# Attention on one core: the order of the next batch's K and Q chunks, and an addition moved from GpSimd to DMA

## The chip, the cores and the metric

The kernel runs on one core of a Trainium2 chip. A core has a matrix engine (TensorE, in the profile PE for matmuls and PEld for the loading of weights), three engines for element-wise work (VectorE, DVE; ScalarE, ACT; GpSimd, POOL), a synchronisation engine (SP) that here only issues DMAs, and 16 DMA engines that all queues share. The engines run their instruction streams in order and wait for each other by semaphores.

The metric is the device time of one execution in microseconds. The kernel before took 791.19 us in the median of three runs (790.79, 791.19 and 791.87).

## The reference

Eight independent batches of softmax attention, 2048 queries and keys, 512 wide, float32 in and out:

```python
scores = np.matmul(q, k.transpose(0, 2, 1)) / np.sqrt(d_k)     # q, k, v: (8, 2048, 512)
attn_weights = special.softmax(scores, axis=-1).astype(np.float32)
return np.matmul(attn_weights, v)
```

## The kernel before

Both matrix products are computed in float16 by Strassen-Winograd recursion: seven products of half-sized blocks instead of eight, with the sums of blocks made by DVE. For the scores the blocks of K are 4 chunks of 512 rows (K0 to K3, the tiles `kraw`), of Q 4 chunks too (two of them form one "sp", half of a batch's queries). For the product with V there is a second level for three of the seven products (class `Fine`, the function `fine`).

**Periods and slots.** The main loop runs over 32 periods g, four to a batch (qt = g % 4, called first to fourth period here). A period has 28 slots, and a slot holds two 512-column score matmuls for the queries to come, together with PV matmuls for the period itself. Everything is laid out by hand by (period, slot): `PRODUCTS` says at which slot a PV product is issued, `SUMS` at which slot DVE gets a sum (`k01@11` is the first sum of chunk K0 at slot 11 of the second period, `q1@25` the first sum of the next queries, `k31@1` the first of K3 in the fourth), and `PLAN` at which slot the next batch's inputs are loaded and transposed. A slot is a place in the engines' instruction streams, not a clock: what stands there may wait.

**Inputs of the next batch.** `load` (L133) is a DMA on the POOL queue that converts 512 rows from float32 in memory to float16 in a tile `stage`; there are two such tiles, so a third load waits until the transposition of the first has finished. `dma_transpose` (L159) is a transposing DMA on the SP queue from `stage` into `kraw` or `qraw`; it waits for its load and until PE has read the old contents for the last time. `load_v` (L220) loads V on the POOL queue. With K's chunks c and j the sums of K are at L194 to L197, those of Q at L211 to L214, of V at L228 to L231, and those for the second level at L602 to L605.

**Outputs.** A period ends in two row blocks, a and b, of four parts each, C11, C12, C21 and C22 (`o11`, `o12`, `o21`, `o22`), 128 x 256 float32 in tiles `o`. There are eight such tiles, and a new one is whichever has come free first. ACT scales a product out of PSUM into an `o` (L460), DVE may add a second part (L463), and SP sends the store (L473). C22 and C21 are finished by products a7, b7, a4 and b4 at the beginning of the next period, C12 by a6 and b6 in slots 19 to 24. C11 is the sum of two scaled parts, done at slots 25 and 27 (`after2`):

```python
way = ADDERS[self.g % NQT]
...
more = self.half()
self.scaled(more, self.y[:, 0:H], self.r1)
if way == "dma":
    nc.gpsimd.dma_start(out=self.o11, in_=more, accum_op=ADD)
    stores.append((clock[0] + LAG, lambda: self.store(self.o11, 0, slice(0, H))))
    return
nc.gpsimd.tensor_add(self.o11, self.o11, more)
```

In the form "pool" POOL adds the parts (L569) and the store follows at once; in the form "dma" a DMA on the POOL queue adds one tile onto the other in place (L564), and the store is put on SP's queue LAG slots later, where it waits for that DMA. The last two periods of all have no scores and no C11 of this kind.

**Queues.** SP's queue carries all stores and all transposing DMAs in the order of the slots, POOL's all loads, the additions and the accumulating DMAs. Each is in order: an instruction that waits holds what stands behind it.

Of the kernel before, what the change touches and what calls it, by code (L numbers as in the profile page):

```python
# [12 lines left out]
def kernel(  # L13
# [394 lines left out]
    spare_halves = deque()  # L408
    stores = deque()
    clock = [0]  # L410
    LAG = 12
    ADDERS = ("pool", "pool", "dma", "dma")

    class Pair:

# [109 lines left out]
    class Fine(Pair):  # L525
# [29 lines left out]
        def after2(self):  # L555
            if "y" in INNER(self.g) and self.g < NP - 2:
                way = ADDERS[self.g % NQT]
                if way == "dve":
                    self.final(self.o11, self.y[:, 0:H], self.r1)
                else:  # L560
# [4 lines that stand above are left out]
                        stores.append(  # L565
                            (clock[0] + LAG, lambda: self.store(self.o11, 0, slice(0, H)))
                        )
# [124 lines left out]
    def INNER(g):  # L692
        return INNERS[g % NQT] if 0 < g < NP - 2 else END_INNERS.get(g, "")
# [69 lines left out]
    PLAN = {}  # L763
    for qt_, slot_, *what_ in (
# [10 lines left out]
    ):  # L775
        PLAN.setdefault((qt_, slot_), []).append(what_)
# [229 lines left out]
```

## Time and profile before

| | |
|---|---|
| median of three runs | 791.19 us (790.79 to 791.87) |
| profiled execution, its own time | 790.61 us |
| its span, first to last instruction | 788.8 us |
| granted TensorE clock, mean | 1.000 |
| PE busy | 782.1 us, 99% of the span |
| DVE busy | 704.8 us, 89% |
| ACT busy | 645.8 us, 82% |
| POOL busy | 125.9 us, 16% |
| memory read and written | 100.73 MB and 33.55 MB |
| C11 added by POOL (L569) | 30 instructions, mean 936 ns |
| C11 added by DMA (L564) | 28 issues of 128 KB, 3.4 us to landing in the median |

The profile is of one execution. A line of a timeline reads: start in us from the first instruction, duration, engine, line of the kernel, operation, what it writes and reads, shape, how many are merged, and in brackets how long the engine stood idle before and what ended that. "SPq" and "POOLq" are entries of a queue rather than work of an engine. A line of the chain of waits has start, length and what ran, or which DMA was waited for. A line "DMA to landing" has the least, median and longest time from issue to landing. A matmul's duration overlaps with the next one's, so steps are read from starts, not from durations.

### The profile page before, as it was taken

To read this page: it belongs to the slowest core of one execution; us is meant where nothing else is said; L and a number is where in the kernel's file an instruction comes from. 1 tells how busy PE (TensorE), PEld (TensorE's weight loads), DVE (VectorE), ACT (ScalarE), POOL (GpSimd) and SP (SyncE) were. 2 spreads that over 40 slices of the span, in tenths; PEclk is the share of its full clock that TensorE was granted. 3 is DMA by queue.
4 is the path that set the end of the run, shared out by engine and by line. 5 is a ranking of instruction groups with operands and counts; after the bars stand their busy time and mean duration, and the time that the engine had idled before them with its cause. 6 is when DMAs were issued, how large, how long until landed. Compare 5 with 4: busy or idle time off the path is not lost.

```text
span 788.8 us, 17985 instructions
## 1 busy us (share of the span) xinstructions
PE 782.1 (99%) x6574; PEld 536.9 (68%) x6574; DVE 704.8 (89%) x1562; ACT 645.8 (82%) x1339; POOL 125.9 (16%) x166
## 2 busy tenths in 40 slices
PE   9999999999999999999999999999999999999998
PEld 5556666666667666666666676676666666667686
DVE  3789999989999899997999989999899988999864
ACT  4678888888888988888888888888888878888852
POOL 4011111121121120211202121022210222100000
PEclk9999999999999999999999999999999999999999
DMA  9999991999939998499966999579992999922112
GB/s 222 182 150 161 181 205 42 195 194 165 196 50 206 199 178 146 84 200 173 185 136 112 191 202 166 111 141 184 188 202 68 160 191 185 175 74 61 49 67 94
DMA packets 210488, 119.73 MB, mean 152 GB/s; under 512 B 124768, under 2 KB 209376, under 8 KB 210400
## 3 DMA queue, kind: packets, MB, share of 16 engines
q0 software_dynamic: 53680, 52.96, 45.4%
q1 hardware_dynamic: 156432, 65.30, 40.2%
q8 instruction: 51, 0.84, 0.4%
q10 hardware_dynamic: 288, 0.33, 0.1%
q14 instruction: 37, 0.30, 0.1%
HBM read 100.73 MB, written 33.55 MB: 170 GB/s over the span
## 4 chain that ended last, share of the span: by engine, by line
PE 96%; DVE 1%; DMA 1%; ACT 1%; issue 0%; DVEq 0%; ACTq 0%
PE t L342 45%; PE t L451 30%; PE t L648 17%; PE t L285 2%; DMA kraw<-stage 1%; PE tr L169 1%; PE t L867 0%; PE tr L146 0%; PE t L301 0%; DVE s L396 0%; DVE cz L367 0%; ACT left L278 0%; ACT o L460 0%; DVE s L398 0%; ACT right L278 0%
## 5 line engine op out<-in xcount | busy, mean ns | idle before, releaser
L460 ACT ACTIVATE o<-t,r 128x256 f32<-128x256 f32 x314 | 143.6, 479 | 84.6 <-DVE r L486 29.6
L342 PE MATMUL t<-qraw,kraw 128*128 128x512 f16 x728 | 198.0, 379 | 0.1
L278 ACT ACTIVATE left<-t 128x512 f16<-128x512 f32 (+1 forms) x260 | 154.2, 600 | 11.7 <-PE t L342 4.7
L342 PE MATMUL t<-qs,ks 128*128 128x512 f16 x488 | 138.7, 379 | 0.1
L278 ACT ACTIVATE right<-cz 128x1024 f16<-128x1024 f32 x122 | 129.8, 1064 | 1.0 <-DVE cz L364 0.8
L342 PEld LDWEIGHTS <-kraw 128*128 128x128 f16 x976 | 87.1, 97 | 57.9 <-issue 0.8
L451 PEld LDWEIGHTS <-right 128*128 128x128 f16 x1024 | 99.6, 98 | 36.3 <-issue 1.5
L451 PEld LDWEIGHTS <-s 128*128 128x128 f16 x1072 | 102.2, 97 | 29.8 <-issue 0.3
L648 PEld LDWEIGHTS <-si 128*128 128x128 f16 x1044 | 76.0, 97 | 38.4 <-DVE si L605 2.5
L342 PEld LDWEIGHTS <-ks 128*128 128x128 f16 x732 | 67.9, 97 | 40.2 <-issue 0.2
L367 DVE TENSOR_TENSOR cz<-t,cz 128x512 f32<-128x512 f32 x122 | 83.5, 685 | 12.0 <-PE t L342 4.1
L358 ACT COPY cz<-t 128x512 f32<-128x512 f32 x120 | 70.4, 587 | 27.0 <-PE t L342 25.5
L364 DVE TENSOR_TENSOR cz<-t,cz 128x512 f32<-128x512 f32 x122 | 83.3, 683 | 6.0 <-PE t L342 5.5
L648 PEld LDWEIGHTS <-left 128*128 128x128 f16 x928 | 66.2, 97 | 20.6
L463 DVE SCALAR_TENSOR_TENSOR o<-t,r,o 128x256 f32<-128x256 f32 x134 | 62.4, 477 | 18.1 <-ACT ci L666 7.2
L353 ACT COPY t<-t 128x512 f32<-128x512 f32 x120 | 70.0, 583 | 3.2 <-PE t L342 0.8
L451 PE MATMUL t<-vt,s 128*128 128x256 f16 (+1 forms) x560 | 72.5, 272 | 0.0
L342 PE MATMUL t<-qs,kraw 128*128 128x512 f16 x244 | 72.5, 378 | 0.0
L342 PE MATMUL t<-qraw,ks 128*128 128x512 f16 x244 | 72.5, 378 | 0.0
L361 ACT COPY cz<-t 128x512 f32<-128x512 f32 x122 | 71.1, 582 | 0.4
L648 PE MATMUL t<-vh,left 128*128 128x128 f16 x696 | 67.3, 219 | 0.0
L451 PE MATMUL t<-vh,s 128*128 128x257 f16 x512 | 67.0, 273 | 0.1
(102 smaller groups left out, 1216.6 us busy)
## 6 DMA issues: line engine op xcount, KB each, us to landing
out_dram<-o SPq DMA_DIRECT2D x256, 128.0 KB, 3.2
vh<-in_v_dram POOLq DMA_DIRECT2D x32, 512.0 KB, 10.6
stage<-in_q_dram POOLq DMA_DIRECT2D x28, 512.0 KB, 7.0
stage<-in_k_dram POOLq DMA_DIRECT2D x28, 512.0 KB, 8.1
o<-o POOLq DMA_DIRECT2D x28, 128.0 KB, 3.4
right<-in_q_dram POOLq DMA_DIRECT2D x2, 512.0 KB, 10.1
right<-in_k_dram POOLq DMA_DIRECT2D x2, 512.0 KB, 12.1
first<-in_q_dram SPq DMA_DIRECT2D x2, 256.0 KB, 3.6
```

The lines of the kernel that those rows point to most:

```text
L278: nc.scalar.activation(out=out_, in_=in_, func=EXP, scale=inv_sqrt_d)
L285: nc.tensor.matmul(st[:], kops[c][0][:, n, dc, :], qraw[0][:, half * NT:(half + 1) * NT, dc, :], start=(dc == 0), stop=(dc == ND - 1),)
L342: nc.tensor.matmul(dst[:], lhs[:, j, dc, :], rhs[:, :, dc, :], start=(n in (1, 5) and dc == 0), stop=(dc == 1), skip_group_check=True,)
L353: f(out=self.y[:], in_=self.x[:])
L358: f(out=self.cz[:, 1, :], in_=self.z[:])
L361: nc.scalar.copy(out=self.cz[:, 0, :], in_=self.x[:])
L364: nc.vector.tensor_add(self.cz[:, 1, :], self.x[:], self.cz[:, 1, :])
L367: nc.vector.tensor_add(self.cz[:, 0, :], self.z[:], self.cz[:, 0, :])
L451: nc.tensor.matmul(dst[:, 0:width], lhs(j), rhs(j), start=(first and j == 0), stop=(j == NJ - 1), skip_group_check=True,)
L460: nc.scalar.activation(out=out_, in_=src, func=COPY, scale=r[:])
L463: nc.vector.scalar_tensor_tensor(out=out_, in0=src, scalar=r[:], in1=out_, op0=MULT, op1=ADD)
L648: nc.tensor.matmul(dst, lhs[:, j, :], rhs[:, j, :], start=(n == 1 and j == 0), stop=(j == NI - 1), skip_group_check=True,)
```

## The change

Two things are changed.

The order of the next batch's inputs in the first two periods. Before: Q's first chunk, Q's second, K0, K1, K2, K3. After: Q's first chunk, K0, Q's second, K1, K2, K3. K0 is loaded at slot 5 of the first period instead of 18 and transposed at its slot 20 instead of slot 0 of the second; Q's second chunk takes K0's old places. K1 to K3, Q's third chunk and V's second are loaded or transposed some slots later.

C11 is added by DMA in all four periods instead of the last two, and LAG is 9 instead of 12. So the store of C11 is issued 9 slots after its addition everywhere: in the first two periods of a batch that is 9 slots later than before, in the other two 3 slots earlier.

On SP's queue K0's transposition now stands between the stores of a6 and b6 in the first period; Q's second chunk is transposed at the start of the second, followed by six stores (a7, b7, a4, b4 and the two C11) where three stood before K1's transposition. In the third period the two C11 stores stand just ahead of K3's transposition. On POOL's queue the accumulating DMAs stand where the additions stood, and K1's load stands behind them. The built program's other orders are unchanged.

```diff
-    LAG = 12
-    ADDERS = ("pool", "pool", "dma", "dma")
+    LAG = 9
+    ADDERS = ("dma", "dma", "dma", "dma")
...
         (0, 0, "load", "q", 0), (0, 10, "trans", "q", 0),
-        (0, 5, "load", "q", 1), (0, 16, "trans", "q", 1),
-        (0, 18, "load", "k", 0), (1, 0, "trans", "k", 0),
-        (0, 24, "load", "k", 1), (1, 8, "trans", "k", 1),
-        (1, 8, "load", "k", 2), (1, 20, "trans", "k", 2),
-        (1, 16, "load", "k", 3), (2, 7, "trans", "k", 3),
-        (2, 0, "load", "q", 2), (2, 14, "trans", "q", 2),
+        (0, 5, "load", "k", 0), (0, 20, "trans", "k", 0),
+        (0, 18, "load", "q", 1), (1, 0, "trans", "q", 1),
+        (1, 3, "load", "k", 1), (1, 12, "trans", "k", 1),
+        (1, 9, "load", "k", 2), (1, 21, "trans", "k", 2),
+        (1, 22, "load", "k", 3), (2, 8, "trans", "k", 3),
+        (2, 2, "load", "q", 2), (2, 14, "trans", "q", 2),
         (2, 15, "load", "q", 3), (2, 26, "trans", "q", 3),
-        (0, 14, "load", "v", 0), (1, 12, "load", "v", 1),
+        (0, 14, "load", "v", 0), (1, 14, "load", "v", 1),
         (2, 6, "load", "v", 2), (2, 20, "load", "v", 3),
```

## The prediction

> **What bounds the kernel now.** I read the page first, then the chain of waits in order of time, then the waits, then the timelines around the places where the chain leaves PE. Page and chain:
>
> ```profile
> span 788.8 us, 17985 instructions
> ...
> PE 782.1 (99%) x6574; PEld 536.9 (68%) x6574; DVE 704.8 (89%) x1562; ACT 645.8 (82%) x1339; POOL 125.9 (16%) x166
> ...
> PE 96%; DVE 1%; DMA 1%; ACT 1%; issue 0%; DVEq 0%; ACTq 0%
> ```
>
> PE is the bound almost everywhere: it is busy 782.1 of 788.8 us and holds 96% of the chain. No edit here touches a matmul, so only the few places where PE stands still can be won, and a new place like them is what can be lost. Eight batches repeat one pattern, so the same piece of the chain, the 16 PV matmuls at the start of a batch's second period, shows each batch's length:
>
> ```profile
> 62.97 1.75 PE t L451 x16
> ...
> 158.49 1.75 PE t L451 x16
> ...
> 253.88 1.75 PE t L451 x16
> ...
> 349.27 1.75 PE t L451 x16
> ...
> 445.51 1.75 PE t L451 x16
> ...
> 540.91 1.76 PE t L451 x16
> ...
> 636.58 1.75 PE t L451 x16
> ...
> 732.63 1.75 PE t L451 x16
> ```
>
> The distances are 95.52, 95.39, 95.39, 96.24, 95.40, 95.67 and 96.05 us. 95.39 is the floor of an undisturbed batch (112 slots, so 0.852 us a slot); above it lie 0.13, 0, 0, 0.85, 0.01, 0.28 and 0.66, together 1.93 us. The largest, from 349.27 on, in the chain, in DVE's timeline and in the waits of the whole run:
>
> ```profile
> 351.09 8.78 DMA kraw<-stage
> ...
> 362.04 0.62 PE t L648 x8
> ```
> ```profile
> 359.89 0.42 DVE L194 TENSOR_TENSOR ks<-kraw 128x512 f16<-128x512 f16 x1 [2.15 <-DMA kraw<-stage]
> ```
> ```profile
> DVE ks L194 <- DMA kraw<-stage: 6.2, 4, 2.1
> ```
>
> K's first chunk is transposed by DMA from 351.09 to 359.87. DVE, free since 357.74, waits 2.15 us for it with its first sum (k01), and the PV sums queued behind k01 on DVE come late, so PE stands until 362.04. It happens in four batches with different lengths; two of them cost PE 0.85 and 0.66, where the chunk lands latest. This is the end that arrives last.
>
> A second loss is small and in each batch. POOL and DVE at the same boundary, one DVE line over the run, and PE after it:
>
> ```profile
> 345.16 0.74 POOL L133 DMA_DIRECT2D stage<-in_k_dram  x1 [15.73 <-DMA qraw<-stage]
> ...
> 348.58 0.92 POOL L569 TENSOR_TENSOR o<-o 128x256 f32<-128x256 f32 x1 [0.45 <-ACT o L460]
> 349.71 0.92 POOL L569 TENSOR_TENSOR o<-o 128x256 f32<-128x256 f32 x1 [0.21 <-ACT o L460]
> ```
> ```profile
> 349.03 1.01 DVE L231 TENSOR_TENSOR vt<-vh,vt 128x1024 f16<-128x1024 f16 x1
> 349.96 0.94 DVE L602 TENSOR_TENSOR si<-s 128x512 f16<-128x512 f16 x1
> ```
> ```profile
> L602 DVE TENSOR_TENSOR si<-s x29: 411/418/944, 63.3 to 733.3; 128x512 f16<-128x512 f16 x29
> L213 DVE TENSOR_TENSOR qraw<-qraw x15: 680/685/1018, 41.1 to 710.0; 128x1024 f16<-128x1024 f16 x15
> ```
> ```profile
> 352.58 0.59 PE L342 MATMUL t<-qraw,kraw 128*128 128x512 f16 x2
> 353.09 1.03 PE L451 MATMUL t<-vt,right 128*128 128x256 f16 x8
> ```
>
> A DVE operation that meets a POOL add takes longer: L602 0.94 where its median is 0.42, L213 up to 1.02 against 0.685, L231 1.01. DVE loses about 0.85 us at the end of a batch's first period and 0.33 at the end of its second. PE feels it once: two 512-column matmuls at 0.216 each should end the step at 353.01, the next starts at 353.09, so 0.08 us, which is inside the 95.39 of each batch; the 0.28 of the batch from 540.91 and the 0.13 of the first are longer cases of it, or of it and the first loss together.
>
> **The change, part by part.** *Adds by DMA.* Thirty POOL adds (0.92 us of POOL each) go; thirty accumulating DMAs come, each an issue on POOL of 0.85. POOL is 16% busy: nothing either way. ACT writes the second part in both forms. What DVE does beside such issues is seen where the kernel has them already, at the end of the fourth period:
>
> ```profile
> 421.84 1.70 POOL L564 DMA_DIRECT2D o<-o  x2 [21.71 <-ACT o L460]
> ```
> ```profile
> 422.34 0.68 DVE L229 TENSOR_TENSOR vt<-vh,vt 128x1024 f16<-128x1024 f16 x1
> 422.94 0.68 DVE L213 TENSOR_TENSOR qraw<-qraw 128x1024 f16<-128x1024 f16 x1
> ```
>
> L213 takes 0.68 there, its undisturbed time. So the slowing goes with the adds: 7 x 0.08 = 0.56 us for PE, and its share of the 0.28 and 0.13.
>
> [...]
>
> *Traffic.* Thirty more transfers of 128 KB.
>
> ```profile
> q0 software_dynamic: 53680, 52.96, 45.4%
> ```
> ```profile
> DMA to landing us min/median/max: 2.6/3.4/7.1
> ```
>
> 45.4% of 788.8 over 53,680 packets is 6.7 ns of all 16 engines per packet. My estimate for an add, 128 rows of 1 KB, is 128 x 6.7 = 0.85 us, so two of them push what is queued behind by up to 1.7 us; the lower bound is nothing, since the queues have gaps. The second row is the landing of the existing adds (L564).
>
> *C11's store.* In the third and fourth periods it is issued 3 slots (2.6 us) earlier, in the first and second 9 slots (7.7 us) later; the number of stores is the same. The store waits for its add to land. In the first period the add is issued where the POOL add stood (348.58), lands by 355.7 at the worst 7.1, and SP reaches the store after 356; no wait. In the second period the adds are issued from slots 25 and 27 on; 0.85 for each issue and at worst 7.1 to landing are 9 to 10 slots, so they may land about a slot (0.85 us) after the stores' turn at slots 6 and 8 of the third period, and K3's transposition, next on SP, is late by that: see its margin below.
>
> *K0 ahead of the second Q chunk.* SP's queue in this stretch, the transposing DMAs of K over the run (time on SP, then landing), the landing of stores, and ACT:
>
> ```profile
> 340.62 3.87 SPq L159 DMA_TRANSPOSE qraw<-stage  x1
> 344.57 6.41 SPq L473 DMA_DIRECT2D out_dram<-o  x4
> 351.09 5.25 SPq L159 DMA_TRANSPOSE kraw<-stage  x1
> 356.43 1.50 SPq L473 DMA_DIRECT2D out_dram<-o  x3
> ```
> ```profile
> L159 SPq DMA_TRANSPOSE kraw<-stage x28: 1772/5274/8046, 63.8 to 666.5; - x28
> ...
> DMA to landing us min/median/max: 5.3/8.5/12.0
> ```
> ```profile
> DMA to landing us min/median/max: 1.7/3.2/8.9
> ```
> ```profile
> 363.79 0.84 ACT L460 ACTIVATE o<-t,r 128x256 f32<-128x256 f32 x2 [0.66 <-DVE r L486]
> ```
>
> K0's load takes the second Q chunk's place, whose data were there by 340.62. Its transposition stands on SP behind a6's store, which SP reached at 344.57; at 345.1 at the latest it is issued, and with 5.3, 8.5 or 12.0 to landing it is done at 350.4, 353.6 or 357.1. DVE wants it at 357.74. Even the worst landing is in time, so the 2.15 goes: 0.85 + 0.66 us of PE, and the remainder of the 0.28 and 0.13. What is late next on DVE is nothing that the waits show.
>
> *The second Q chunk in K0's place.* Its load waits for the same stage buffer as K0's did (15.73 us on POOL, to 345.16), lands by 351.09, up to 352.8 with the traffic above, and its transposition keeps SP 5.25. Its sums are at slot 25 of the period, 21 us after slot 0: hidden. But SP is in order, and behind it now stand six stores instead of three. In the second period the buffer that ACT takes for C12 (the first of the two in the row at 363.79) used to be freed by C11's store, sent before the transposition; now it is freed by a7's store, sent behind it. That store starts at 356.43 to 358.1 and lands 3.2 later, 359.6 to 361.3; without K0's wait ACT wants the buffer at 363.79 - 0.85 = 362.94. Cost nothing, margin 1.6 to 3.3 us; with 8.05 on SP after 352.8 it would be 1.1 us late.
>
> *The other moves.* K1 is transposed 30 slots (25.6 us) before its sums, K2 24 slots, K3 21 slots (17.9 us), against 12.0 to landing: hidden. K1's load waits for K0's transposition to free its buffer, as it did for the Q chunk's. V1's load keeps its place between K2 and K3 on POOL. At the end, the last two adds land at least 2.6 us after issue where POOL took 0.92; neither PE nor the last store waits for them.
>
> **The sum.** 1.93 + 0.56 = 2.49 us off the profiled execution: 790.61 - 2.49 = 788.1 (span 786.3). The median of the three runs, 791.19, is 0.58 above that execution. If that is more waiting of the same kind, which varies from batch to batch, it goes too; if it is not, 788.7. I take the middle, 788.4, with 787.7 to 789.4 as this case's own range.
>
> **The rivals.**
> - *SP becomes the wait (slower).* The Q chunk's transposition holds SP past ACT's margin, so a7's store frees the buffer late, and ACT delays PE. It decides once SP is free later than 359.7 (362.94 - 3.2), which needs 6.9 to 8.6 us there beside the median of 5.27; for it speaks that six stores now queue behind it and DMA is near full, against it that K0's own transposition at the same place let SP go at 356.3. Price as for K0, 0.85 in six batches: 788.4 + 5.1 = 793.5.
> - *K0 stays late.* K0's transposition and the Q chunk's load now run together and slow each other. Only the DVE part is won: 0.56 + 0.41 = 1.0, from the median 790.2. Against it: 12.0 to landing would still do.
> - *DMA issues hold DVE like the adds.* The 0.56 and 0.41 are not won, 1.51 is: from the median 789.7. Against it: 0.68 at 422.94.
> - *The change does not do what it says.* The stalls it removes are replaced by as many elsewhere (K3 behind C11's stores, ACT's buffers): 790.3 to 791.5.
>
> **How the numbers follow.** The forecast 0.64; SP the wait 0.12; K0 late 0.08; DVE held 0.08; nothing won 0.08. 0.2% is 1.6 us, about what a measurement tells here (the runs spread over 1.08). Faster than 789.6: the forecast and half of "DVE held" and a little, 0.69; within: 0.19; slower: 0.12. The range 787.6 to 791.4 takes in all but the slower rival and small tails.
>
> **What would show it.** Right: no row of DVE L194 waiting for kraw<-stage; the seven distances of the chain all 95.3; L602 and L231 without values near 0.94 and 1.01; PE's busy time nearly unchanged and a span of 786 to 787. Wrong: a wait of ACT o L460 for out_dram<-o, or of L194, in the second period of a batch; L602 still at 0.94 beside L564; C11's stores in the third period holding K3's transposition so that L194 waits there.

## The result, and the profile after

The changed kernel is slower: 799.1 us in the median of six runs against 791.63 in six runs of the kernel before, ratio 1.0102 [1.0081, 1.0123]. The forecast was 788.4. (Ratios, here and below, leave out runs over 1.5% above the fastest of the same kernel, which can take away a kernel's own longest runs too; medians are over all runs, of which one of e9 took 1669 us and one of e11 2928.) The profiled execution took 799.29 us. From the page of the changed kernel, the span, the engines, and the chain of waits by engine and by line:

```profile
span 797.5 us, 18034 instructions
...
PE 782.7 (98%) x6574; PEld 538.1 (67%) x6574; DVE 697.8 (88%) x1562; ACT 643.3 (81%) x1339; POOL 124.3 (16%) x166
...
PE 89%; DMA 8%; ACT 1%; issue 1%; DVE 0%; SPq 0%; POOL 0%; POOLq 0%; ACTq 0%; DVEq 0%
```

PE's work is the same (782.7 against 782.1), but DMA holds 8% of the chain where it held 1%. The same piece of the chain as in the prediction, once per batch (start, length, what ran):

```profile
62.91 1.75 PE t L451 x16
...
158.21 1.75 PE t L451 x16
...
254.27 1.75 PE t L451 x16
...
351.67 1.75 PE t L451 x16
...
452.09 1.75 PE t L451 x16
...
549.46 1.75 PE t L451 x16
...
644.77 1.75 PE t L451 x16
...
741.16 1.75 PE t L451 x16
```

The distances are 95.30, 96.06, 97.40, 100.42, 97.37, 95.31 and 96.39. An undisturbed batch is now 95.30, where it was 95.39: the forecast 0.08 per batch is there. But five batches are longer, by 0.76, 2.10, 5.12, 2.07 and 1.09, together 11.14 us (0.01 in a sixth). Against the 1.93 that went and 7 x 0.09 = 0.63, that is 8.6, the growth of the span (8.7). No row of DVE L194 waiting for kraw<-stage is left. What has come instead, from the waits of the whole run (total, times, longest):

```profile
ACT o L460 <- DMA out_dram<-o: 9.5, 6, 3.9
...
PE t L648 <- ACT ci L666: 6.7, 4, 3.3
...
ACT o L460 <- DMA o<-o: 4.8, 3, 2.4
```

ACT waits for a free `o` tile, either until a store has read it (out_dram<-o) or until an accumulating DMA has (o<-o), and PE waits for what ACT does next. There are three places.

**Adds held on POOL** (batches with 0.76, 2.07, 1.09). The chain, and POOL's timeline:

```profile
466.30 12.49 DMA kraw<-stage
...
480.05 9.23 DMA o<-o
...
490.05 0.38 PE t L648 x4
```
```profile
479.32 0.74 POOL L133 DMA_DIRECT2D stage<-in_k_dram  x1 [11.62 <-DMA kraw<-stage]
480.05 1.82 POOL L564 DMA_DIRECT2D o<-o  x2
```

K3's load stands at slot 22, the adds of the second period at slots 25 and 27, so behind it on POOL. The load waits 11.62 us for K1's transposition to free its stage buffer. The adds go out at 480.05, 5.2 us into the third period (3.8 and 3.9 in the other two of these batches; in the batches behind the first where K3's load is not late, 0.8 to 1.0 for the first add and 2.2 for the second), and need 9.23 to land. ACT reuses their tiles at 12.2 us into the period; here it gets them 2.3 us later.

In the old kernel K3's load (slot 16) stood ahead of the additions too, but out of their way. The same place of the same batch there:

```profile
461.26 0.74 POOL L133 DMA_DIRECT2D stage<-in_k_dram  x1 [4.48 <-DMA kraw<-stage]
469.06 1.13 POOL L569 TENSOR_TENSOR o<-o 128x256 f32<-128x256 f32 x1 [7.05 <-issue]
```

What has moved is K1's transposition, for which the load waits. It starts some 5 us later than before; it landed 2.5 to 3.9 us into the third period in these three batches, and 1.4 to 8.7 us ahead of it in every batch of the old kernel.

**A store behind K2's transposition** (the batch with 5.12). SP's timeline and the chain:

```profile
373.98 4.15 SPq L159 DMA_TRANSPOSE kraw<-stage  x1
378.22 9.42 SPq L473 DMA_DIRECT2D out_dram<-o  x6
```
```profile
378.22 8.19 DMA out_dram<-o
...
388.61 0.39 PE t L648 x4
```
```profile
DMA to landing us min/median/max: 11.0/11.0/11.0
```

K2's transposition (slot 21) was issued at 373.98 and took 11.0 us to land, to 384.96 (last row: its own landing). The last store of the second period, b6's, stands right behind it, was issued at 378.22 and landed at 386.41; the quickest store of the run lands in 1.7 us. ACT needed that tile 3.85 us earlier. The store landed 1.45 us after the transposition ahead of it; that the one held the other is the author's reading of this, which e9 below puts to a test.

The transposition also starts later than it did. K2's load now waits on POOL for the second Q chunk's transposition (11.41 us here, to 365.40), and K2's transposition waits for the load: behind the first batch it is issued between 2.3 us before the third period and 0.2 us into it, in the old kernel 3.9 to 4.3 us before it.

**Stores behind the second Q chunk's transposition** (the batch with 2.10). The same at the head of the second period, where the six stores stand behind that transposition:

```profile
263.46 7.46 DMA out_dram<-o
```

### The profile page after: what moved, and what is told of

Same layout as the page of the kernel before. It is cut to its first block, busy times and chain, and to the rows that moved or that the text cites. A ratio compares the mean times of both kernels' runs of the same rounds, so it can differ in the third digit from the quotient of the medians.

```text
span 797.5 us, 18034 instructions
## 1 busy us (share of the span) xinstructions
PE 782.7 (98%) x6574; PEld 538.1 (67%) x6574; DVE 697.8 (88%) x1562; ACT 643.3 (81%) x1339; POOL 124.3 (16%) x166
## 3 DMA queue, kind: packets, MB, share of 16 engines
q0 software_dynamic: 58000, 56.90, 49.2%
## 4 chain that ended last, share of the span: by engine, by line
PE 89%; DMA 8%; ACT 1%; issue 1%; DVE 0%; SPq 0%; POOL 0%; POOLq 0%; ACTq 0%; DVEq 0%
PE t L342 42%; PE t L451 28%; PE t L648 16%; DMA kraw<-stage 3%; DMA o<-o 2%; PE t L285 2%; DMA out_dram<-o 2%; PE tr L169 1%; DMA first<-in_q_dram 1%; PE t L301 0%; PE tr L146 0%; ACT right L278 0%; ACT cz L358 0%; ACT left L278 0%; ACT o L460 0%
## 5 line engine op out<-in xcount | busy, mean ns | idle before, releaser
L451 PEld LDWEIGHTS <-right 128*128 128x128 f16 x1024 | 99.7, 98 | 35.5
L451 PEld LDWEIGHTS <-s 128*128 128x128 f16 x1072 | 102.3, 97 | 29.8 <-issue 0.2
L367 DVE TENSOR_TENSOR cz<-t,cz 128x512 f32<-128x512 f32 x122 | 83.6, 685 | 26.2 <-ACT cz L361 12.2
L564 POOL DMA_DIRECT2D o<-o x58 | 50.5, 895 | 243.3 <-ACT o L460 195.2
L451 PE MATMUL t<-vt,s 128*128 128x256 f16 (+1 forms) x560 | 72.5, 273 | 0.0
## 6 DMA issues: line engine op xcount, KB each, us to landing
right<-in_q_dram POOLq DMA_DIRECT2D x2, 512.0 KB, 10.1
```

The source lines that it names most:

```text
L367: nc.vector.tensor_add(self.cz[:, 0, :], self.z[:], self.cz[:, 0, :])
L451: nc.tensor.matmul(dst[:, 0:width], lhs(j), rhs(j), start=(first and j == 0), stop=(j == NJ - 1), skip_group_check=True,)
```

## The experiments

Five theories were set against each other. A: the second period's adds are held on POOL behind K3's load. B: the new order of loads crowds by itself. C: the added transfers cost by their traffic. D: C11's stores stand in the wrong place. E: the transposition ahead of the stores lands late in the filled queues, and the tiles come free late. A and E have their places above; the runs had to say which of the edits bring them.

| run | edit | median us | ratio to before |
|---|---|---|---|
| e1 | order only | 791.27 | 0.9993 [0.9972, 1.0014] |
| e2 | adds and stores only | 794.67 | 1.0057 [1.0029, 1.0086] |
| e3 | changed, K3's load behind the adds | 801.77 | 1.0105 [1.0053, 1.0157] |
| e4 | changed, LAG 12 | 804.8 | 1.0100 [1.0061, 1.0139] |
| e5 | changed, second period's adds on POOL | 795.01 | 1.0045 [1.002, 1.007] |
| e6 | changed, first period's adds on POOL | 801.88 | 1.0126 [1.0109, 1.0143] |
| e7 | changed, both on POOL, stores still 9 slots later | 793.16 | 1.0032 [1.0002, 1.0061] |
| e8 | changed, both added by DVE, LAG 12 | 792.7 | 1.0022 [1.0006, 1.0038] |
| e9 | changed, K2's transposition behind b6's store | 799.49 | 1.0043 [0.9995, 1.0091] |
| e10 | e9 and e3 together | 790.42 | 0.9993 [0.9967, 1.0018] |
| e11 | e1 with K2's transposition as in e9 | 795.63 | 1.0046 [1.0025, 1.0067] |
| e12 | changed, plain copies for adds | 803.08 | 1.0103 [1.0033, 1.0173] |
| e13 | e10 and the Q chunk's transposition behind five stores | 790.05 | 1.0000 [0.9975, 1.0026] |
| e14 | e13 with POOL adds | 793.88 | 1.0044 [1.0013, 1.0075] |
| e15 | e13 with V1's load later | 803.63 | 1.0148 [1.0123, 1.0173] |
| e16 | changed, V1's load later | 809.99 | none |
| e17 | e13 with V1's load later still | 792.15 | 1.0019 [0.9999, 1.0039] |
| e18 | e13 again, one run | 788.09 | none |

### Which half of the change: e1, e2

```diff
e1: the order of after, and
+    LAG = 12
+    ADDERS = ("pool", "pool", "dma", "dma")
e2: PLAN of before, and LAG 9 with four "dma"
```

> Only the order of the K, Q and V loads and transpositions is changed; C11 is added as before (POOL, POOL, DMA, DMA; LAG 12). Theory A (the accumulating DMAs of the second period stand on POOL's queue behind K3's load, which waits for K1's transposition; they land with K3's packets some 9 us after issue, and ACT waits for the tiles they hold): a POOL add in that place frees its tiles 0.9 us after K3's load is issued, so the stops of PE in the third period, 0.76, 2.08 and 1.09 us in the changed kernel, go, K0's wait stays away: 789.5 to 792. Theory B (the new order itself crowds DMA and SP, so stores land late whatever adds C11): PE still stops 1 to 3.5 us in several batches: 795 to 800.

> Only C11's addition is changed (DMA in all periods, LAG 9); loads and transpositions stand as before, so K3's load is issued at about 42 us of a batch, ahead of the adds of 49 us. Theory A: the adds are not held, no stop in the third period; DVE's operations at 0.94 and 1.01 beside POOL adds go back to 0.42 and 0.68; K0's wait stays: 789 to 791.5. Theory C (the extra 30 transfers of 128 KB crowd the queues by themselves): ACT waits for stores, 793 to 798.

The order alone makes no difference to the median: theory B falls. Its trace (span 787.4, the fastest of its ten runs) has no K0 wait in any batch and keeps the 0.08 us per batch. The adds and stores alone cost 0.57%: there K0's old wait grows, from 6.2 us in total before to

```profile
DVE ks L194 <- DMA kraw<-stage: 11.8, 6, 3.8
```

A part of this is DVE, which without the POOL adds is free for k01 at 9.05 us into the second period instead of 9.50. But the two batches in which PE feels the wait lose 3.82 and 1.64 us to it, where they lost 0.85 and 0.66, and K0 lands up to 12.8 us into the second period (11.6 before). So each half wins its own piece, and in the old order the adds make the K0 wait worse.

### Which part of the adds: e3 to e8

```diff
e3:  (1, 22, "load", "k", 3)  ->  (2, 0, "load", "k", 3)
e4:  LAG = 12
e5:  ADDERS = ("dma", "pool", "dma", "dma")
e6:  ADDERS = ("pool", "dma", "dma", "dma")
e7:  ADDERS = ("pool", "pool", "dma", "dma"), their stores appended with LAG 9
e8:  ADDERS = ("dve", "dve", "dma", "dma"), LAG = 12
```

> The changed kernel with one entry moved: K3's load at slot 0 of the third period instead of slot 22 of the second, so that it stands behind the two adds on POOL's queue; it is issued no later, since it waits for K1's transposition either way. Theory A: the adds are issued at 48.7 and 49.9 us of a batch and land some 3 to 5 us later; the stops of 0.76, 2.08 and 1.09 us go; those in the third and fourth batch that show a store as the last arrival may stay: 791 to 796. Theory B or C: as the changed kernel, 798 to 800.

> The changed kernel with LAG back at 12: C11's stores three slots later, in the third period behind K3's transposition on SP instead of ahead of it. Theory A: ACT waits for tiles that the adds free, not the stores of C11: as the changed kernel, 798 to 800. Theory D (C11's stores, waiting on SP for late adds, hold the stores and K3's transposition behind them, and that delays ACT): 2 to 5 us less, 793 to 797.

> The changed kernel with C11 added by POOL in the second period again; DMA adds in the first, third and fourth, LAG 9. Theory E (the transfers of the adds fill DMA queues that are nearly full, the transposition ahead of the stores on the hardware queue lands late, and the stores that free ACT's tiles land with it): the two adds of the first period alone delay the second Q chunk and K1, K2; some stops remain where a store is the last arrival (third period): 791 to 797. Theory A (it is the two adds of the second period, held behind K3's load): as the order alone, 789.5 to 791.5.

> The changed kernel with C11 added by POOL in the first period again; DMA adds in the second, third and fourth, LAG 9. Theory A: all of the loss stays, 797 to 800. Theory E: a part stays, since the second period's adds still load the queues where K2 is transposed, but K1 and K2 start earlier: 792 to 797. If 789.5 to 791.5, the first period's adds are the cause.

> The changed kernel with POOL adds in the first two periods, but C11's stores left where the change puts them, 9 slots after the add. Neither traffic nor a held add, only the placing of the stores. Theories A and E: 789.5 to 791.5, as the order alone. Theory D (the stores in the changed places free ACT's tiles late): 795 to 800.

> The changed order, C11's second part added by DVE in one operation (0.48 us, as it does for C12) in the first two periods, by DMA in the others with LAG 12. No extra transfers, no POOL operation beside DVE. Theories A and E: no stop from tiles, and DVE gains 1.2 us of slowing a batch and pays 4 x 0.48 us: 788 to 791. If DVE has no room there (11.9 us busy of 12 in the stretch before): 791 to 794.

e3 takes away what holds the adds, and the run is no faster: A alone falls. No ACT wait for o<-o is left in its trace (the longest of its four runs), but the stores behind K2's transposition are late in three batches instead of one. Its chain in the batch of 378.22 above:

```profile
378.36 7.00 DMA out_dram<-o
```

e6, with only the second period's adds by DMA, costs as much as the whole change; e5, with only the first period's, 0.45%; e7, with the same order and the late stores but no added transfers, 0.3%. So D is small (and e4's later stores did not help: 1.0100), and most of the loss comes with the second period's two transfers of 128 KB. In e6 they are not held on POOL (issued 1.1 to 1.5 us into the third period), so they cost by another way as well. It is seen on K2's transposition. Counted from the start of the third period, it landed at 3.5 to 5.5 us in e7's seven batches, 0.4 to 8.0 in e1's, both without added transfers, and at 1.8 to 12.5 in e6's. The new order alone thus comes near the 8.5 us at which ACT takes the tile of the store behind it, and with the transfers the landing goes past that. In e6's sixth batch it started at 569.60, and its landing took

```profile
DMA to landing us min/median/max: 12.5/12.5/12.5
```

with the two adds issued 1.1 and 2.2 us behind it. e8 has no ACT wait on tiles, but DVE's own adds stop PE by some 0.24 us twice in a batch.

### Both places at once: e9, e10, e11

```diff
e9:  (1, 21, "trans", "k", 2)  ->  (1, 25, "trans", "k", 2)
e10: e9, and (1, 22, "load", "k", 3)  ->  (2, 0, "load", "k", 3)
e11: e9's edit on e1
```

> The changed kernel with K2's transposition four slots later (slot 25 instead of 21), so that the second period's last store (b6) is sent ahead of it instead of behind it. [...] Theory E (the store behind the transposition frees the tile late): the stop of 3.46 us in the fourth batch and its half clock go, no ACT L460 wait for out_dram<-o above 0.5 us in a third period; theory A's part (the adds behind K3's load, some 0.8 + 2.1 + 1.1 us in three batches) stays, since K2's transposition does not touch that load: 793.5 to 796. Theory A alone (all comes from the adds behind K3's load) or C (traffic alone): 798 to 800, as the changed kernel. If K2's own transposition now comes too late for its sums, DVE L194 waits for kraw<-stage in the third period and it is slower than 800.

> The changed kernel with both: K2's transposition at slot 25 and K3's load at the third period's slot 0, behind the adds on POOL. If the late store (E) and the held adds (A) together are the whole loss: no wait of ACT L460 for o<-o and none above 0.5 us for out_dram<-o, 788 to 791, and faster than the kernel before by what was forecast or a part of it. If the adds' transfers cost by their traffic alone (C): 795 or more, with waits elsewhere, since the same bytes move in the same stretch.

> The new order of loads with the adders and the stores' delay of before (the run that stood level with the kernel before), and K2's transposition at slot 25. Theory E: what spread that run from 789.3 to 795.5 are the same late stores, so this one stands at 789 to 790 with its runs closer together. Theory B (the new order crowds by itself, wherever the transposition stands): 791 to 792 with the same spread.

e9 sends b6's store ahead of K2's transposition. In the batch where that store had been the delay, the chain now goes through the adds:

```profile
367.41 10.22 DMA kraw<-stage
...
378.90 12.57 DMA o<-o
```

So A and E hide behind each other: repaired alone, the other ends last in the same batch (this one in e9; in e3 the batch that had lost 1.09 to the adds now waits for a store). e9's own runs, from 789.69 to 802.22, leave open whether it gained. Repaired together (e10), the loss is gone: 790.42, ratio 0.9993, and ACT's waits in the third periods with it. What is left in its trace is one stop of 4.4 us, at the third place (that batch lost 6.3: behind the stop eight matmuls of L451 took 1.71 us, 0.87 ahead of it, and the mean granted clock of that execution was 0.998):

```profile
ACT o L460 <- DMA out_dram<-o: 8.6, 3, 5.8
```
```profile
263.60 8.48 DMA out_dram<-o
...
273.52 1.15 PE t L342 x4
```

e11 missed: with the POOL adds and the stores of before, K2's transposition then stands behind C11's first store as well and starts 2.3 us into the third period. Its trace has one stop of 3.0 us, in a fourth period, where ACT waits for a store issued at 203.44 right behind a Q chunk's transposition.

### Traffic or addition: e12

```diff
-    nc.gpsimd.dma_start(out=self.o11, in_=more, accum_op=ADD)
+    nc.gpsimd.dma_start(out=self.o11, in_=more)
```

> The changed kernel with each accumulating transfer of C11's parts replaced by a plain copy of the same 128 KB (the first part is overwritten, so the sum is left out). The bytes, the issues on POOL, the order and the waits stay. If it is the traffic and the order (C, A, E): 798 to 800, the same stops. If it is the reading and adding that makes these transfers slow: they land in less than half the time in the third period (below 5 us after issue where they take 5 to 11), K2's transposition lands by 6 us into the third period, and the time is 791 to 795.

This kernel leaves the sum out. The time stays, as far as four runs from 794.18 to 806.29 tell (the trace is of the longest), and the landings over the run too:

```profile
DMA to landing us min/median/max: 1.9/5.9/10.0
```

The changed kernel has 2.6, 5.9 and 10.8. So nothing here points to the reading and adding as what makes these transfers slow or costly, rather than where and among what they stand.

### The third place, and whether the gain is there: e13, e14, e18

```diff
e13: e10, and (1, 0, "trans", "q", 1)  ->  (1, 7, "trans", "q", 1)
e14: e13 with ADDERS = ("pool", "pool", "dma", "dma")
e18: e13 once more
```

> The run with K2's transposition at slot 25 and K3's load behind the adds, and now the second Q chunk's transposition at slot 7 of the second period instead of slot 0, so that five of the six stores go out on SP ahead of it. If the stops of 2 to 4.4 us in the second period (third batch in the changed kernel and in three of the experiments) come from those stores standing behind the Q chunk's transposition: no wait of ACT L460 for out_dram<-o above 0.5 us in a second period, runs close together, 788 to 789.5, and faster than the kernel before (ratio 0.996 to 0.998). If they come from the filled queues wherever the stores stand: the stop comes back in some runs (794 and more) and the median stays at 790.4.

> The same with C11's parts of the first two periods added on POOL again, the stores still 9 slots later. The POOL adds then slow DVE's operations beside them: if the forecast's 0.08 us per batch is all that this costs, 0.5 to 0.7 us above the run without them, with some 0.08-us stops of PE at each batch's first period and rows of L602 or L231 near 0.94 and 1.01; if the transfers cost more than the slowing, it stands below that run.

> The kernel with the three placements once more, for a second trace: its first trace had no stop at all (788.4), while half of its runs took 790 to 800. If those runs are longer by the same cause as in the changed kernel (stores or K2's transposition landing late beside loads), this trace has either no stop again and 787.5 to 789, or, if it is longer than 789.5, the difference stands in one or two waits of ACT L460 for out_dram<-o or of DVE for a transposed chunk, behind a load or transposition that landed 2 us or more later than in the first trace. If it is longer without such a wait, the spread has another cause.

Both traces of this kernel have no stop at all. Span of e13, the chain by engine, the piece of the chain in the first two batches and the last, and the landings of K's transpositions:

```profile
span 786.6 us, 18013 instructions
...
PE 98%; DMA 1%; ACT 1%; DVE 0%; issue 0%; SPq 0%; ACTq 0%
```
```profile
63.45 1.75 PE t L451 x16
...
158.75 1.75 PE t L451 x16
...
730.56 1.75 PE t L451 x16
```
```profile
DMA to landing us min/median/max: 4.3/7.2/10.1
```

Seven batches of 95.30 (730.56 - 63.45 = 667.11 = 7 x 95.30), 788.36 us in e13's trace and 788.09 in e18's (span 786.3). That is the forecast (span 786.3, time 788.1 to 788.7), so the two gains are real and of the forecast size. But they are not reliable: e13's twelve runs go from 787.7 to 800.8, with a median of 790.05, and it can't be told from the kernel before (whose runs beside it went from 789.65 to 795.69). e14 brings the POOL adds back, and with them sends C11's stores of the first two periods at once: the edit does not keep them 9 slots later, as the expectation says it does. The 0.08-us stops return in the second periods, its trace has two more stops of 0.4 and 1.0 us, and it stands at 793.88. K2's transposition then stands behind a store of C11, as in e11, and starts 2.3 us into the third period, so its time is not the price of the POOL adds alone.

### The traffic itself: e15, e16, e17

```diff
e15: e13 with (1, 14, "load", "v", 1) -> (2, 18, "load", "v", 1), (2, 15, "load", "q", 3) -> (2, 22, "load", "q", 3)
e16: the same two on the changed kernel
e17: e13 with (1, 14, "load", "v", 1) -> (2, 19, "load", "v", 1)
```

> The run with all three placements (K2's transposition at slot 25, K3's load behind the adds, the second Q chunk's transposition at slot 7), and now 1 MB less in the crowded stretch: V1's load goes from the second period's slot 14 to the third period's slot 18, and the fourth Q chunk's load to slot 22 behind it. If what still spreads that run (787.7 to 800.8) is crowding of the DMA engines in the second and third periods: K2's transposition lands by 4 us into the third period, all runs within 2 us, median 788 to 789, faster than before (0.996 to 0.998). If it is not the traffic there: the same spread, 790. If V1 now lands behind its sums (12.8 us into the fourth period) or K3's transposition behind its own: DVE waits there and it is slower, 791 to 793.

> The changed kernel with only V1's and the fourth Q chunk's loads later, every place of the change kept. If the traffic in the stretch is what makes the transposition, the stores behind it and the adds land late (C, E): landing of K2's transposition down from 5 to 10 us into the third period to below 5, the loss at least halved: 791 to 795. If only the places on the queues matter (adds behind K3's load, stores behind transpositions): K1's transposition and K3's load stand as they did, the same stops, 797 to 800.

> The run with all three placements and V1's load (1 MB) from the second period's slot 14 to the third period's slot 19, behind the fourth Q chunk's load, which waits on POOL for the stage buffer that K3's transposition frees; so it starts at some 69 us of the batch, when K3's transposition is done, and not beside it as in the run before. If the traffic beside a transposition is what makes it and the stores behind it late: K2's transposition lands by 4 us and K3's by 20 us into the third period, no wait of ACT L460 for out_dram<-o, the runs close together at 788 to 789.5, ratio 0.996 to 0.998. If the spread of the runs has another cause: 790 with the same spread. If V1 and V3, now loaded together, land behind their sums (12.8 and 13.6 us into the fourth period): DVE waits for vh<-in_v_dram there and it is 791 or more.

With V1's load out of the second period, K2's transposition lands at 3.1 to 4.7 us into the third period in all of e15's batches (4.2 to 9.9 in e13). But three loads of V now go out together beside K3's transposition. POOL, SP, and that transposition's landing in the batch above:

```profile
382.53 2.23 POOL L220 DMA_DIRECT2D vh<-in_v_dram  x3
```
```profile
389.34 7.67 SPq L159 DMA_TRANSPOSE kraw<-stage  x1
```
```profile
DMA to landing us min/median/max: 14.3/14.3/14.3
```
```profile
ACT o L460 <- DMA out_dram<-o: 24.7, 12, 3.2
```

K3's transposition takes 14.3 us here and up to 17.0 in other batches (8.5 to 10.1 in e13), the stores behind it are late (in four batches DVE waits for the chunk too, up to 0.9 us), and every batch loses 1.2 to 2.9 us, in its fourth period. So the mechanism of E can be moved to another place by moving traffic beside another transposition. e16's four runs lie between 795.17 and 815.82, and it settles nothing. e17 puts the load where no transposition of K runs: K2's lands at 3.1 to 4.8 us in six batches. In the third batch the second Q chunk's load and K0's transposition, which start together, both take 11 us, in the five batches after the first 7 to 9; everything behind is late, and the trace has stops of 2.2 and 0.6 us. The median, 792.15, is no better than e13's: the traffic of V1 is not what spreads the runs.

## Why the prediction was wrong

**K0 ahead of the second Q chunk: right.** The wait is gone wherever the new order stands (changed kernel, e1, e13), and with it PE's stops there.

**Adds by DMA instead of POOL: right for DVE.** From the changed kernel's groups of DVE by shape:

```profile
L602 DVE TENSOR_TENSOR si<-s 128x512 f16<-128x512 f16 x29 | 12.1, 417 | 0.2
...
L231 DVE TENSOR_TENSOR vt<-vh,vt 128x1024 f16<-128x1024 f16 x16 | 10.9, 680 | 0.0
...
L213 DVE TENSOR_TENSOR qraw<-qraw 128x1024 f16<-128x1024 f16 x15 | 10.2, 681 | 0.0
```

Before, their means were 544, 840 and 816 ns. The longest of each is now 426, 683 and 685 ns, where it was 944, 1240 and 1018. The trace shows no issue that holds DVE, so the rival "DMA issues hold DVE" falls for these operations.

**C11's store: the step that failed first.** "In the second period the adds are issued from slots 25 and 27 on" overlooked that K3's load stands ahead of them on POOL and waits for K1's transposition, which the change itself makes later. In the three batches the adds left 3.8 to 5.2 us into the third period and landed after 9.2 to 9.5 us, not "at worst 7.1". The sentence named SP's next transposition as the one that would be late; the one that waits is ACT, for the adds' tiles. Worth 0.76 + 2.07 + 1.09 = 3.9 us of the trace.

**The other moves: "hidden" was asked of the wrong reader.** K2's transposition was measured against its sums 24 slots on, and they are never late. But on SP b6's store stands behind it, and ACT takes that tile 8.5 us into the third period. In the old kernel K2's transposition landed at 1.1 to 4.8 us there, and what the change does to it was not asked: the load behind the Q chunk's transposition, the two added transfers beside it. Worth 5.12 us in one batch here; in e6 the same wait stands in four batches. The same question was not asked of K1, whose landing lets K3's load and the adds go.

**Traffic: mis-sized, and in the wrong quantity.** 49.2% of 797.5 less 45.4% of 788.8 is 34.3 us of all 16 engines for thirty adds, 1.14 us each, not 0.85, if the whole growth of the queue is put on them; an add has 144 packets there (4,320 more for thirty), not 128. Small, but the delay that counted is not this sum: with the two adds beside it K2's transposition landed as late as 12.5 us into the third period (e6), without them at 8.0 at the latest (e1, e7).

```profile
q0 software_dynamic: 58000, 56.90, 49.2%
```

**The rival "SP becomes the wait" came too**, with the place and the buffer as described, but it cost PE 2.10 us in one batch, not 0.85 in six. In two others ACT waited there too, 0.88 and 1.10 us, without stopping PE: the forecast's margin of 1.6 to 3.3 us was used up in three batches. "K0 stays late" fell with the first point. "The change does not do what it says" named ACT's buffers as a place where stalls could come back, and they did, but it priced them at about as much as was won (790.3 to 791.5), where 11 us came.

**The sum.** 2.49 was right as the gain of these edits where nothing else waits: the traces of e13 and e18 show it. The missing terms were +11.14, 9.04 at the first two places and 2.10 at the third. They come from where the added transfers, a load and the stores stand on two queues. Two moved entries (e10) take back the first two places; the third is gone in the traces of e13 and e18 only, where the Q chunk's transposition is moved too. What lengthens about half of e13's runs is open: neither of its traces shows such a run.

## What to carry to other kernels

When a step on an in-order queue is moved, list who stands behind it on that queue and which engine needs that one next, not only who reads the step's own result: here the victims were an output store behind a transposition and an addition behind a load. When two such delays sit in the same stretch, repairing one can show little or nothing (e3, e9), because the other ends at nearly the same time; test them together before a theory is dropped. And where the DMA engines are busy for 90% of the time (here 90.9%, the sum of the queues' shares in the changed kernel's page), a margin taken from landings in the old kernel is not a bound for the new one.

## What had not been expected of the chip

**The clock after a stop.** The stop at 386 cost more than its own length. Windows of the changed kernel (stretch, length, busy time of PE, PEld, DVE, ACT and POOL, granted clock, DMA share, GB/s):

```profile
386.00:388.50 2.50, 0.00 (x0) 0.00 (x0) 0.08 (x1) 2.00 (x5) 1.11 (x2) 1.00 1.04 213
...
390.00:392.00 2.00, 2.00 (x9) 0.88 (x8) 0.97 (x4) 1.23 (x5) 0.00 (x0) 0.50 1.08 182
392.00:394.00 2.00, 2.00 (x18) 1.72 (x17) 1.25 (x4) 0.58 (x2) 0.00 (x0) 0.74 1.21 219
```

After PE had stood for 3.46 us, to 388.61 (3.29 of them in the timeline's own count of idle time), it ran for 1.01 us at the full clock; then the granted clock was 0.50 for 3.41 us (389.62 to 393.03), which makes the other 1.66 us of the batch's 5.12. Behind the two next longest stops of the same trace, with 1.94 us of idle time up to 271.95 and 1.91 up to 490.05, the granted clock was 1.00. How long a stop must be to cost the clock is not shown. No margin in the prediction had this cost.

**Landings late together.** Stores of 128 KB, of which the quickest land in 1.7 us, took 5.6 to 8.5 us where the chains of the changed kernel (8.19 and 7.46), of e3 (7.28, 7.00 and 5.60) and of e10 (8.48) wait for them. A transposition stood ahead of each on SP's queue; the two of the changed kernel landed 1.45 and 1.98 us after it. The landing of one transposition of K, between 4.3 and 17.0 us in e13 and e15, moves with what else is loaded at that time, as K3's shows: 8.5 to 10.1 in e13, 14.3 to 17.0 beside three loads of V in e15.
